# Input projection in three passes, the last of two k groups in one sum; modulation and gates ahead of it; weight offsets by kind

## The chip, the cores and the metric

The kernel runs on one core of a Trainium2 chip. The metric is the time that the device takes for one execution, in microseconds (us). Three runs of the kernel before took 1610.08, 1606.48 and 1610.29 us, a median of 1610.08. The engines are PE (TensorE, with PEld for its weight loads), DVE (VectorE), ACT (ScalarE), POOL (GpSimd) and SP (SyncE, which here only issues DMAs).

## The reference, cut to what matters

Two transformer blocks follow each other, for 256 tokens of width 2048, all in fp32. The change touches the first block only, apart from the place of weights in SBUF, which holds for all weights.

```
c_act = silu(c)
mod = c_act @ w_ada + b_ada                  # 2048 x 6144; c is one vector
shift, scale, gate = split(mod, 3)
h = rms(x) * (1 + scale) + shift             # 256 x 2048
proj = h @ w_in                              # 2048 x 8192
a_q, a_k, a_v, a_z, g_q, g_f, g_i, g_z = split(proj, 8)     # 1024 columns each
att = chunk_attention(a_q, a_k, a_v, bias) * silu(a_z)      # 8 heads, masked bias
hg  = hgrn2(g_q, g_f, g_i) * silu(g_z)                      # recurrence over tokens
x = x + gate * (concat(att, hg) @ w_out)
# second block: pool mixer, MLA, memory attention, w_o; then a gated FFN with 5632 columns
```

The sum over the 2048 rows of `w_in` is cut into four k groups of 512 rows. k group kg needs only the 512 columns kg of `h`, and so only these columns of `shift` and `scale`.

## The kernel before, in words

**Weights.** `load` (line 105) fetches a weight tile of 1 MB, 128 x 2048 fp32, into one of three buffers `wr`. `split_w` (line 112) cuts it, half a tile at a time, into a high part `wh` (ACT cast, line 120, three buffers) and a low part `wl` (DVE subtraction, line 121, two buffers). `tile_mm` (line 140) makes a job of each half tile: three matmuls for each product (line 165), high by high, high by low and low by high. There are three kinds. In T the weights are PE's stationary operand and 256 tokens move, in N the activations are stationary and 512 weight columns move, and in T2 (the FFN's gate and up weights and the like) the weights are stationary and 512 and 256 columns move. Two dummy tiles of 64 bytes, `pada` and `padb`, stand before and between `wh` and `wl` in SBUF; their addresses are the same for all three kinds.

**Order of the rest.** Everything that is not a weight job lies in two queues, `evq` and `bgq`, and is issued after each job until a budget of the phase is used up (`BUDGET`, line 34, `drain`); `AHEAD` says how many jobs are split ahead of the one whose matmuls are issued. So the program's order on each engine is set when it is built.

**Passes.** Twelve of the sixteen groups of `w_in` (512 columns each, `first_groups`, line 621) go through four passes, one for each k group: 48 tiles, 96 jobs. Each tile has PSUM banks of its own, and `part` (line 626) takes them to SBUF: for kg 0 an ACT copy (line 632), for kg 1 to 3 a DVE addition to what is there (line 634). `after` (line 811) runs behind each tile. It also advances the modulation of the next k group: two groups of 512 columns of `w_ada` (a scale and a shift, four 1 MB tiles each), `ada_steps` (line 402). Each tile has four chunks of 128 x 512 elements (`ada_tile`, line 368): "V" is one DVE operation, multiply and add (line 382), "P" is a product on ACT into `pts` (line 387) and an addition on POOL (line 388); the first chunk of a sum has no addition. `PAIR` = ("PPPP", "VVVV") gives the plan of the two groups. `ada_sum` (line 391) adds over partitions with small matmuls into a PSUM tile `ax`. At the end of a pass `make_h` (line 429) makes the next 512 columns of `h`, with their high and low parts.

**Gates.** The four groups 8 to 11 of `w_ada` (the block's `gate`) begin behind tile 10 of pass 3 (`GSTART`) with plans of three V and one P, the last all V. Their tiles are loaded with `load` into the weights' own `wr` buffers. They go on, a step per tile, through the stages gz (groups 14 and 15 of `w_in`), az (6 and 7) and out (`w_out`), where `need_y` (line 919) finishes them when needed.

**Beside it.** The recurrence of `hgrn2` (`level_inputs`, line 665, and on) begins once the four g_q and g_f groups are complete, in the fourth tile of pass 3; the attention heads (`chunk_heads`, line 640) once their groups are, from tile 8 on. A 128 x 128 mask `maskB` is added on POOL to each head's bias (line 646).

Of the kernel before, what the change touches and what calls it, by code (L numbers as in the profile page):

```python
# [28 lines left out]


# [28 lines left out]
def trunk_kernel(ctx, tc, a, out):  # L59
# [231 lines left out]
    maskB = sp_.tile([P, P], F32, tag="maskB", name="maskB")  # L291
    scanm = sp_.tile([P, T], F32, tag="scanm", name="scanm")
# [61 lines left out]
    n_ada = [0]  # L354

    def ada_buf(ng):
        if ng % 4 == 0 and ng < 8:
# [8 lines left out]
        return None
# [247 lines left out]
    def load_masks():  # L614
        for t, n in ((maskB, "maskB"), (scanm, "scanm")):
            SP.dma_start(t, a[n])
        hgf = slot("s7", [P, len(LEVELS), T])
        SP.dma_start(hgf, a["hgm"])
        later(1, lambda: V.tensor_copy(hgm, hgf))
# [188 lines left out]
    gates, xp = gate_steps(), []  # L808
    steps, hgt = [], []

    def after(kg, n, banks, ng, mode, dst, g, fin):
        for i, b in enumerate(banks):
            later(0.6, lambda i=i, b=b: part(kg, ng, mode, dst, g, b, i, fin), evq)
        if n == 0:
            steps.append(ada_steps((4 + kg + 1, kg + 1), PAIR) if kg < 3 else gates)
        if (n % 4 < EARLY and (kg < 3 or n >= GSTART)):
            next(steps[-1], None)
# [7 lines left out]
        if kg < 3 and n == 11:  # L825
            for _ in steps[-1]:
                pass
            make_h(kg + 1)
            if kg == 2:
                t = ytile("y0")  # L830
                hgt.extend((t[:, 0], t[:, 1]))
# [534 lines left out]
def _constants():  # L1366
# [11 lines left out]
    maskB = np.where(i[None, :] // 64 <= i[:, None] // 64, 0.0, NEG).astype(f)  # L1378
# [3 lines left out]
    for li, m in enumerate(LEVELS):  # L1382
# [7 lines left out]
        "maskC": maskC, "maskB": maskB, "scanm": scanm,  # L1390
# [60 lines left out]
```

## Time and profile before

| | |
|---|---|
| median of three runs | 1610.08 us (1606.48 to 1610.29) |
| profiled execution | 1608.93 us |
| its span | 1607.2 us |
| mean granted clock of PE | 0.991 |
| PE busy | 1549.3 us, 96% |
| DVE busy | 1157.4 us, 72% |
| ACT busy | 860.0 us, 54% |
| POOL busy | 366.9 us, 23% |
| DMA | 331.75 MB, mean 206 GB/s |

The span runs from the first to the last instruction of the profiled execution; 1.73 us of the execution's time lie outside it. By the first and last weight jobs of each part the stages are, in us from the start of the span: the memory's projection 10.2 to 88.2, pass 0 to 165.9, pass 1 to 235.5, pass 2 to 307.4, pass 3 to 394.0, gz to 472.0, az to 533.7, out to 638.6, then the second block, whose feed-forward runs from 882.7 to the end. A window by these bounds gives each engine's busy time in a stage. A busy PE is not PE at its peak, so its time is compared with what the number of jobs asks for.

### The profile page before, as it was taken

What the parts mean: (1) busy time and instruction counts of PE and PEld (TensorE: products, weight loads), DVE (VectorE), ACT (ScalarE), POOL (GpSimd) and SP (SyncE); (2) the same over time, 40 slices, a digit from 0 to 9 for tenths busy, and PEclk for the clock granted to TensorE, in tenths of its full rate; (3) what the DMA queues carried; (4) which work ended last, traced back from release to release, by engine and by line L of the source; (5) the groups of instructions that cost most, each with busy time, mean ns of one, the idle gap of its engine ahead of it and who ended that gap; (6) DMA issues with size and microseconds to landing.
All of it is one profiled execution on the core that took longest, in us unless ns stands there. A gap on an engine that the chain in (4) does not pass through costs nothing.

```text
span 1607.2 us, 24896 instructions
## 1 busy us (share of the span) xinstructions
PE 1549.3 (96%) x9754; PEld 1391.6 (87%) x9754; DVE 1157.4 (72%) x1610; ACT 860.0 (54%) x1254; POOL 366.9 (23%) x363
## 2 busy tenths in 40 slices
PE   5789999999899999999999999999999999999999
PEld 4677988878898999987999888888888888888887
DVE  7776999899997769567667766776676677545444
ACT  6366655564556745367645555555555555333332
POOL 3533435156653011512101211111111111000000
PEclk9899999999999999999999999999999999999999
DMA  9568878453655467443435555555555555556653
GB/s 386 211 245 300 339 286 318 180 183 132 229 191 213 175 243 264 158 163 136 153 132 184 184 188 202 187 194 200 186 200 192 190 204 183 203 190 208 206 189 131
DMA packets 50949, 331.75 MB, mean 206 GB/s; under 512 B 5648, under 2 KB 8080, under 8 KB 13456
## 3 DMA queue, kind: packets, MB, share of 16 engines
q1 hardware_dynamic: 50832, 330.17, 57.1%
q8 instruction: 76, 1.25, 0.3%
q14 instruction: 41, 0.34, 0.1%
HBM read 328.05 MB, written 2.10 MB: 205 GB/s over the span
## 4 chain that ended last, share of the span: by engine, by line
PE 83%; DVE 9%; POOL 2%; issue 2%; ACT 2%; DMA 1%; SPq 0%; DVEq 0%; ACTq 0%; POOLq 0%
PE mm L165 78%; DVE wl L121 4%; DVE acc L382 2%; POOL acc L388 1%; PE ax L724 1%; DMA wr<-in_w_mem_kv_dram 1%; PE ax L397 1%; ACT wh L120 1%; DMA wr<-in_w_ada_dram 1%; PE ax L253 1%; PE ax L522 1%; PE ax L223 0%; PE ax L514 0%; DVE s L314 0%; PE ax L650 0%
## 5 line engine op out<-in xcount | busy, mean ns | idle before, releaser
L121 DVE TENSOR_TENSOR wl<-wr,wh 128x1024 fp32r<-128x1024 f32 (+2 forms) x516 | 669.6, 1299 | 346.7 <-PE mm L165 308.9
L120 ACT CAST wh<-wr 128x1024 fp32r<-128x1024 f32 (+2 forms) x516 | 534.2, 1038 | 472.8 <-PE mm L165 392.2
L165 PE MATMUL mm<-h,wh 128*128 128x512 f32 (+1 forms) x2560 | 691.4, 343 | 0.4 <-ACT wh L120 0.4
L165 PE MATMUL mm<-h,wl 128*128 128x256 f32 x1984 | 553.5, 279 | 7.5 <-DVE wl L121 7.3
L165 PEld LDWEIGHTS mm<-h,wh 128*128 128x128 f32 x2560 | 444.1, 189 | 56.6 <-ACT wh L120 1.0
L165 PEld LDWEIGHTS mm<-h,wl 128*128 128x128 f32 x1984 | 374.2, 189 | 9.5 <-DVE wl L121 9.3
L165 PE MATMUL mm<-f,wh 128*128 128x512 f32 x704 | 239.4, 389 | 0.0
L165 PE MATMUL mm<-wh,h 128*128 128x512 f32 (+1 forms) x704 | 222.1, 391 | 0.0
L165 PE MATMUL mm<-f,wl 128*128 128x256 f32 x704 | 194.4, 276 | 0.0
L165 PE MATMUL mm<-y,wh 128*128 128x256 f32 x1024 | 185.3, 283 | 0.0
L165 PEld LDWEIGHTS mm<-y,wh 128*128 128x128 f32 x1024 | 156.6, 188 | 0.3 <-ACT wh L120 0.3
L165 PEld LDWEIGHTS mm<-wh,h 128*128 128x128 f32 x704 | 131.2, 188 | 29.1
L165 PEld LDWEIGHTS mm<-f,wh 128*128 128x128 f32 x704 | 132.1, 188 | 27.3
L165 PE MATMUL mm<-y,wl 128*128 128x256 f32 x512 | 143.9, 282 | 2.6 <-DVE wl L121 2.6
L165 PE MATMUL mm<-wl,h 128*128 128x512 f32 (+1 forms) x352 | 137.8, 392 | 3.4 <-DVE wl L121 3.4
L165 PEld LDWEIGHTS mm<-f,wl 128*128 128x128 f32 x704 | 132.2, 188 | 0.0
L1288 POOL TENSOR_TENSOR gp<-sg,R 128x256 f32<-128x256 f32 x44 | 35.9, 818 | 314.3 <-DVE sg L1287 314.3
L388 POOL TENSOR_TENSOR acc<-acc,pts 128x512 f32<-128x512 f32 x45 | 73.6, 1636 | 114.9 <-ACT pts L387 99.4
L165 PEld LDWEIGHTS mm<-y,wl 128*128 128x128 f32 x512 | 96.0, 188 | 3.4 <-DVE wl L121 3.4
L165 PEld LDWEIGHTS mm<-wl,h 128*128 128x128 f32 x352 | 66.3, 188 | 18.7 <-DVE wl L121 5.9
L165 PE MATMUL mm<-wh,s 128*128 128x512 f32 x128 | 45.4, 435 | 10.2 <-ACT wh L120 10.2
L634 DVE TENSOR_TENSOR s<-mm,s 128x512 f32<-128x512 f32 x72 | 49.0, 680 | 2.1 <-PE mm L165 1.8
(305 smaller groups left out, 1557.7 us busy)
## 6 DMA issues: line engine op xcount, KB each, us to landing
wr<-in_w_in_dram SPq DMA_DIRECT2D x76, 1024.0 KB, 4.9
wr<-in_w_gate_dram SPq DMA_DIRECT2D x44, 1024.0 KB, 4.7
wr<-in_w_up_dram SPq DMA_DIRECT2D x44, 1024.0 KB, 4.9
wr<-in_w_down_dram SPq DMA_DIRECT2D x40, 1024.0 KB, 4.9
y<-in_w_ada_dram SPq DMA_DIRECT2D x28, 1024.0 KB, 7.4
wr<-in_w_ada_dram SPq DMA_DIRECT2D x16, 1024.0 KB, 4.8
wr<-in_w_out_dram SPq DMA_DIRECT2D x16, 1024.0 KB, 4.7
wr<-in_w_o_dram SPq DMA_DIRECT2D x16, 1024.0 KB, 4.8
```

Of the source, the lines that this page charges most:

```text
L120: S.copy(hi, raw[:, k : k + n, :])
L121: V.tensor_tensor(lo, raw[:, k : k + n, :], hi.bitcast(F32), ALU.subtract)
L165: PE.matmul(d, l, r, start=st and i == 0, stop=sp and i == len(trip) - 1, skip_group_check=True)
L253: PE.transpose(ps[:, j * T + tb * P : j * T + tb * P + P], d[:, j, tb * P : tb * P + P], ident)
L382: V.scalar_tensor_tensor(accs[0], raw[:, k, :], cc, accs[0], ALU.mult, ALU.add)
L388: G.tensor_tensor(accs[1], accs[1], t, ALU.add)
L397: PE.matmul(ps[:, j * P : j * P + P], acc[:, j * P : j * P + P], ones, start=i == 0, stop=i == len(accs) - 1, skip_group_check=True)
L522: PE.matmul(po[:, :T], vblk(0), t[:, :T], start=True, stop=False, skip_group_check=True)
L634: V.tensor_tensor(d, b, d, ALU.add)
L724: PE.matmul(ps[:, j, b, :], k2[:, j, s], q2[:, j, s], start=True, stop=True)
L1288: G.tensor_tensor(gp[:, 2:], s, R3, ALU.mult)
```

## The change

The change has five parts.

1. *Three passes.* Passes kg 0 and kg 1 remain, 12 tiles each. Then tiles 0 to 2 run with kg 2, tiles 0 to 2 with kg 3, and each of tiles 3 to 11 with kg 2 and kg 3 one after the other. In these 24 tiles kg 2 and kg 3 add up in the same PSUM banks, and `part` takes only the whole sum: the 24 additions of kg 2 are gone. All 24 have the phase "pass3" with its budget of 2.0; pass 2 had 0.5 before.
2. *Modulation ahead.* `chain_steps` runs the modulations of k groups 1, 2 and 3 one after the other within the passes kg 0 and kg 1, two steps behind each fourth tile and one behind the others. Plans are PPPP and VVVV for the first, PPPP and VVPP for the second and third. `modulated` finishes what is left before a k group is first used.
3. *Gates ahead.* Behind the chain, one step per tile, with plan VVPP for all four and with two load buffers of their own in the tile `y1` (`gate_raw`) instead of `wr`. They must be complete before the first head is gated (`gate`, the new assertion), and the waits in `need_y` are gone.
4. *Masks.* The bias mask becomes an addition of a constant on a 64 x 64 corner; `scanm` is kept as bytes and cast beside `hgm`.
5. *Weight offsets by kind.* `wh` and `wl` are tiles of 1024 + 64 elements, and the weights begin at an offset set by `PLACE`. By the addresses that result, modulo 256 bytes and against the activations, before `wh` lies 64 bytes below and `wl` at 0 for all kinds; after, for N both lie at 0, for T both 64 bytes above, for T2 as before.

```diff
+PLACE = dict(N=dict(wh=0, wl=0), T=dict(wh=16, wl=16), T2=dict(wh=48, wl=0))
...
-GATES = ("VVVP", "VVVP", "VVVP", "VVVV")
-PAIR = ("PPPP", "VVVV")
-
-EARLY = 3
-GSTART = 10
+GATES = ("VVPP", "VVPP", "VVPP", "VVPP")
+PAIRS = (("PPPP", "VVVV"), ("PPPP", "VVPP"), ("PPPP", "VVPP"))
...
-        hi = wpool.tile([P, n, cw], F32R, tag="wh", name="wh", bufs=3)
...
-        lo = wpool.tile([P, n, cw], F32R, tag="wl", name="wl", bufs=2)
+        def place(tag, bufs):
+            o = PLACE[mode][tag]
+            t = wpool.tile([P, 1024 + 64], F32R, tag=tag, name=tag, bufs=bufs)
+            return t[:, o : o + n * cw].rearrange("p (k c) -> p k c", k=n)
+
+        hi, lo = place("wh", 3), place("wl", 2)
...
         raw = ada_buf(ng)
-        if raw is None:
-            raw = load(a["w_ada"][ng, kg], 4, 512)
-        else:
-            SP.dma_start(raw, a["w_ada"][ng, kg].rearrange("p (k c) -> p k c", k=4))
+        SP.dma_start(raw, a["w_ada"][ng, kg].rearrange("p (k c) -> p k c", k=4))
...
-                G.tensor_tensor(biases[h][:, P:T], biases[h][:, P:T], maskB, ALU.add)
+                G.tensor_scalar(biases[h][0:64, T - 64 : T], biases[h][0:64, T - 64 : T], NEG, None, ALU.add)
...
+    def chain_steps():
+
+        for kg in range(1, 4):
+            yield from ada_steps((4 + kg, kg), PAIRS[kg - 1])
+            make_h(kg)
+            done.add(f"m{kg}")
+            yield
+        t = ytile("y0")
+        hgt.extend((t[:, 0], t[:, 1]))
+        t = ytile("y1")
+        gate_raw.extend(t[:, i].rearrange("p (k a) t -> p k (a t)", k=4) for i in range(2))
+        done.add("chain")
...
     def after(kg, n, banks, ng, mode, dst, g, fin):
-        for i, b in enumerate(banks):
-            later(0.6, lambda i=i, b=b: part(kg, ng, mode, dst, g, b, i, fin), evq)
-        if n == 0:
-            steps.append(ada_steps((4 + kg + 1, kg + 1), PAIR) if kg < 3 else gates)
-        if (n % 4 < EARLY and (kg < 3 or n >= GSTART)):
-            next(steps[-1], None)
+        if kg != 2:
+            for i, b in enumerate(banks):
+                later(0.6, lambda i=i, b=b: part(kg, ng, mode, dst, g, b, i, fin), evq)
+        if "chain" in done:
+            next(gates, None)
+        else:
+            for _ in range(2 if n % 4 == 0 else 1):
+                next(chain, None)
...
-    for kg in range(4):
-        phase[0] = "pass3" if kg == 3 else "pass0"
-        for n, (ng, mode, dst, g, fin) in enumerate(first_groups):
-            banks = []
-            tile_mm(a["w_in"][ng, kg], 4 * kg, 4, 512, mode, banks, acth, True, True,
...
+    seq = [(n, kg) for kg in range(2) for n in range(12)]
+    seq += [(n, kg) for kg in (2, 3) for n in range(3)] + [(n, kg) for n in range(3, 12) for kg in (2, 3)]
+    open_banks, begun = {}, set()
+    for n, kg in seq:
+        phase[0] = "pass3" if kg >= 2 else "pass0"
+        ng, mode, dst, g, fin = first_groups[n]
+        banks = open_banks.setdefault((n, min(kg, 2)), [])
+        tile_mm(a["w_in"][ng, kg], 4 * kg, 4, 512, mode, banks, acth, kg < 3, kg != 2,
+                pre=(lambda kg=kg: modulated(kg)) if kg and kg not in begun else None,
...
     def need_y(kg):
         for j in range(4 * kg, 4 * kg + 4):
             ensure(f"y{j}")
-        if kg == 2 and not xp:
-            while "g9" not in done:
-                next(gates)
-                drain(0.1)
         if kg == 1 and not xp:
-            while "g10" not in done:
-                next(gates)
-                drain(0.1)
```

**Where instructions move.** First ACT in pass 0: `pts` are products of chunks (line 387 before, 380 after), CAST of `wh` is the weights' (line 120, now 119), COPY takes a tile's bank to `s` (line 632, now 625). Before:

```order
L387 ACTIVATE pts<-y_95,cact 128x512
L120 CAST wh<-wr 128x1024
L387 ACTIVATE pts<-y_95,cact 128x512
L632 COPY s_591<-mm 128x4x128
L120 CAST wh<-wr 128x1024
L632 COPY s_591<-mm 128x4x128
L120 CAST wh<-wr 128x1024
L387 ACTIVATE pts<-y_95,cact 128x512
L120 CAST wh<-wr 128x1024
L387 ACTIVATE pts<-y_95,cact 128x512 x3
```

After:

```order
L380 ACTIVATE pts<-y_94,cact 128x512 x4
L625 COPY s_588<-mm 128x4x128
L119 CAST wh<-wr 128x1024 x2
L625 COPY s_588<-mm 128x4x128
L380 ACTIVATE pts<-y_93,cact 128x512 x2
L380 ACTIVATE pts<-y_94,cact 128x512 x4
L119 CAST wh<-wr 128x1024 x2
L380 ACTIVATE pts<-y_93,cact 128x512 x2
L119 CAST wh<-wr 128x1024 x5
```

Single products and short runs stood between the casts; now runs of four and of six products of the two groups stand there with no cast between them.

Next POOL where the recurrence begins: R, `t_` and the 128 x 512 sums of `s_` are the recurrence's (lines 590 to 711 before, 583 to 704 after), and the additions of a buffer and `pts` are chunks (line 388, now 381). Before:

```order
L676 TENSOR_TENSOR R<-s_2858 128x2x64
L590 TENSOR_TENSOR s_593<-s_593,s_2857 128x512
L675 TENSOR_TENSOR R<-t_3000,s_2858 128x2x64
L692 TENSOR_TENSOR R<-s_2858 128x4x64
L590 TENSOR_TENSOR s_593<-s_593,s_2857 128x512 x3
L711 TENSOR_TENSOR y_2580<-s_592,R 128x2x128
L711 TENSOR_TENSOR y_2580<-s_592,R 128x4x64
```

After:

```order
L381 TENSOR_TENSOR y_2129<-y_2129,pts 128x512 x10
L583 TENSOR_TENSOR s_590<-s_590,s_2640 128x512 x2
L668 TENSOR_TENSOR R<-t_2878,s_2641 128x2x64
L669 TENSOR_TENSOR R<-s_2641 128x2x64
L685 TENSOR_TENSOR R<-s_2641 128x4x64
L381 TENSOR_TENSOR y_2129<-y_2129,pts 128x512 x2
L583 TENSOR_TENSOR s_590<-s_590,s_2640 128x512 x2
L381 TENSOR_TENSOR y_2129<-y_2129,pts 128x512 x2
L704 TENSOR_TENSOR y_2129<-s_589,R 128x2x128
```

Chunk additions of the gates now stand among the recurrence's first operations on POOL, where there were none.

Last SP, the DMA issues around the gates: `wr<-in_w_in_dram` is a tile of `w_in`, `in_w_ada_dram` one of the gates', `bias` the first heads' bias. Before:

```order
L645 DMA bias<-in_rel_dram 128x256 x2
L107 DMA wr<-in_w_in_dram 128x2048 x13
L107 DMA wr<-in_w_ada_dram 128x2048
L107 DMA wr<-in_w_in_dram 128x2048
L107 DMA wr<-in_w_ada_dram 128x2048
```

After:

```order
L107 DMA wr<-in_w_in_dram 128x2048 x4
L638 DMA bias<-in_rel_dram 128x256 x2
L107 DMA wr<-in_w_in_dram 128x2048
L367 DMA y_2130<-in_w_ada_dram 128x2048
L107 DMA wr<-in_w_in_dram 128x2048
```

The gates' tiles went into `wr`, in turn with the weights; now they go into a buffer of `y1` (here `y_2130`), the weights keep `wr` to themselves, and the first stands one weight tile behind the first `bias` instead of thirteen.

## Rows read from the trace of the kernel before

**Rows 1.** The page's first part: busy time, share, instructions
```profile
PE 1549.3 (96%) x9754; PEld 1391.6 (87%) x9754; DVE 1157.4 (72%) x1610; ACT 860.0 (54%) x1254; POOL 366.9 (23%) x363
```

**Rows 2.** Windows, passes 0 to 3, gz, az, out; us, engines, PEclk, DMA, GB/s
```profile
88.20:165.90 77.70, 72.55 (x409) 61.67 (x410) 56.90 (x63) 53.69 (x82) 27.84 (x20) 1.00 0.74 276
165.90:235.50 69.60, 69.60 (x402) 60.51 (x401) 65.22 (x74) 37.29 (x46) 25.99 (x16) 1.00 0.85 320
235.50:307.40 71.90, 70.14 (x401) 60.51 (x400) 63.38 (x77) 34.46 (x40) 26.21 (x17) 1.00 0.70 265
307.40:394.00 86.60, 82.37 (x506) 71.49 (x504) 82.20 (x125) 54.79 (x75) 41.51 (x42) 1.00 0.44 158
394.00:472.00 78.00, 71.46 (x571) 70.31 (x570) 74.71 (x108) 40.54 (x62) 47.83 (x46) 0.93 0.57 203
472.00:533.70 61.70, 58.56 (x487) 57.10 (x485) 48.56 (x88) 40.06 (x62) 19.63 (x17) 1.00 0.58 210
533.70:638.60 104.90, 103.04 (x848) 101.36 (x846) 82.82 (x138) 59.36 (x98) 13.36 (x15) 1.00 0.64 232
```

**Rows 3.** The same windows, instructions of tile ax alone; PE, PEld, DVE, ACT
```profile
235.50:307.40 71.90, 2.10 (x16) 2.09 (x16) 0.31 (x2) 0.00 (x0) 1.00 0.70 265
307.40:394.00 86.60, 15.32 (x120) 14.93 (x120) 9.13 (x15) 1.97 (x4) 1.00 0.44 158
394.00:472.00 78.00, 24.45 (x186) 22.63 (x185) 12.71 (x24) 3.25 (x6) 0.93 0.57 203
472.00:533.70 61.70, 14.59 (x102) 11.92 (x100) 5.11 (x12) 7.38 (x12) 1.00 0.58 210
533.70:638.60 104.90, 13.73 (x79) 11.34 (x76) 5.06 (x13) 5.90 (x14) 1.00 0.64 232
```

**Rows 4.** Pieces of the chain of waits: start us, us, what
```profile
356.33 1.78 PE ax L724 x16
...
418.55 2.83 PE mm L165 x24
```

**Rows 5.** Groups on DVE in pass 1: busy us, mean ns | idle before
```profile
L121 DVE TENSOR_TENSOR wl<-wr,wh 128x1024 fp32r<-128x1024 f32 x24 | 35.1, 1463 | 3.9 <-PE mm L165 1.6 <-issue 1.0 <-ACT wh L120 0.7
L634 DVE TENSOR_TENSOR s<-mm,s 128x512 f32<-128x512 f32 x22 | 15.0, 680 | 0.4 <-PE mm L165 0.4
L382 DVE SCALAR_TENSOR_TENSOR s<-y,cact,s 128x512 f32<-128x512 f32 x15 | 12.0, 802 | 0.1
```

**Rows 6.** The same view for POOL and for ACT
```profile
L388 POOL TENSOR_TENSOR acc<-acc,pts 128x512 f32<-128x512 f32 x16 | 26.1, 1634 | 41.9 <-ACT pts L387 41.1
...
L387 ACT ACTIVATE pts<-y,cact 128x512 f32<-128x512 f32 x15 | 10.4, 717 | 3.4 <-POOL acc L388 2.8 <-DMA y<-in_w_ada_dram 0.6
```

**Rows 7.** Timeline in pass 1: start us, us, engine line op [idle before]
```profile
186.50 1.22 DVE L121 TENSOR_TENSOR wl<-wr,wh 128x1024 fp32r<-128x1024 f32 x1
...
193.53 4.89 POOL L388 TENSOR_TENSOR acc<-acc,pts 128x512 f32<-128x512 f32 x3 [1.51 <-ACT pts L387]
...
197.17 2.33 DVE L121 TENSOR_TENSOR wl<-wr,wh 128x1024 fp32r<-128x1024 f32 x1 [0.67 <-ACT wh L120]
```

**Rows 8.** The chain of waits from gz to out, shares by line
```profile
by line: PE mm L165 50.8%; DVE acc L382 7.9%; DVE wl L121 6.9%; issue 4.1%; DMA wr<-in_w_ada_dram 3.9%; PE ax L724 2.7%; PE ax L397 2.7%; PE ax L650 2.2%; PE ax L253 2.0%; DVE y L725 1.6%; PE ax L522 1.5%; DVE h L314 1.3%; DVE x L908 1.1%; 
```

**Rows 9.** One line's instructions: ns min/median/max, first and last start
```profile
L388 POOL TENSOR_TENSOR acc<-acc,pts x45: 1276/1359/2212, 91.6 to 277.7; 128x512 f32<-128x512 f32 x45
```

**Rows 10.** Timeline of PE in pass 1, then in the feed-forward
```profile
210.26 0.63 PE L165 MATMUL mm<-wh,h 128*128 128x512 f32 x2
210.73 0.40 PE L165 MATMUL mm<-wl,h 128*128 128x512 f32 x1
...
1150.14 0.39 PE L165 MATMUL mm<-h,wh 128*128 128x512 f32 x1
1150.37 0.28 PE L165 MATMUL mm<-h,wl 128*128 128x256 f32 x1
1150.48 0.39 PE L165 MATMUL mm<-h,wh 128*128 128x512 f32 x1
```

More of the change, by code (lines that the diff above doesn't have):

```diff
@@ L290, in trunk_kernel @@
     sp_ = b1.enter_context(tc.tile_pool(name="s", bufs=1))
-    maskB = sp_.tile([P, P], F32, tag="maskB", name="maskB")
-    scanm = sp_.tile([P, T], F32, tag="scanm", name="scanm")
+    scanm = sp_.tile([P, T], U8, tag="scanm", name="scanm")
     hgm = sp_.tile([P, len(LEVELS), T], U8, tag="hgm", name="hgm")
@@ L614, in load_masks @@
     def load_masks():
[L615 to L619, printed above, removed]
+        n = len(LEVELS)
+        hgf = slot("s7", [P, n + 1, T])
+        SP.dma_start(hgf[:, 0:n, :], a["hgm"])
+        SP.dma_start(hgf[:, n, :], a["scanm"])
+        later(1, lambda: (V.tensor_copy(hgm, hgf[:, 0:n, :]), V.tensor_copy(scanm, hgf[:, n, :])))
     first_groups = [(10, "T", gk, 0, none), (11, "T", gk, 1, none), (8, "T", gq, 0, none),
@@ L795, in gate_acc2 @@
     def gate_acc2(ng):
-        if ng < 10:
-            return flat(hgt[0][:, 6:8, :])
-        return slot("s4", [P, 512]) if ng == 10 else tmp([P, 512], "acc2", 1)
+        return flat(hgt[0][:, 6:8, :])
     def gate_steps():
         for ng in range(8, 12):
-            while ng == 11 and not xp:
-                yield
             yield from ada_steps((ng,), (GATES[ng - 8],))
@@ L806, in gate_steps, with modulated @@
                 yield
-    gates, xp = gate_steps(), []
-    steps, hgt = [], []
-    def after(kg, n, banks, ng, mode, dst, g, fin):
-        for i, b in enumerate(banks):
-            later(0.6, lambda i=i, b=b: part(kg, ng, mode, dst, g, b, i, fin), evq)
-        if n == 0:
-            steps.append(ada_steps((4 + kg + 1, kg + 1), PAIR) if kg < 3 else gates)
-        if (n % 4 < EARLY and (kg < 3 or n >= GSTART)):
-            next(steps[-1], None)
+    def chain_steps():
[9 more added lines that the diff above has]
+        done.add("chain")
+    gates, chain, xp = gate_steps(), chain_steps(), []
+    hgt = []
+    def modulated(kg):
+        while f"m{kg}" not in done:
+            next(chain)
+        if kg == 3:
+            for _ in chain:
+                pass
+    def after(kg, n, banks, ng, mode, dst, g, fin):
+        if kg != 2:
[6 more added lines that the diff above has]
+                next(chain, None)
         if kg == 1 and n == 2:
@@ L824, in after @@
             when((f"aq{4 * i}", f"aq{4 * i + 2}", f"ak{4 * i}", f"ak{4 * i + 2}", f"in{4 + i}"), lambda: chunk_heads(i))
[L825 to L831, printed above, removed]
-    for kg in range(4):
-        phase[0] = "pass3" if kg == 3 else "pass0"
-        for n, (ng, mode, dst, g, fin) in enumerate(first_groups):
-            banks = []
-            tile_mm(a["w_in"][ng, kg], 4 * kg, 4, 512, mode, banks, acth, True, True,
-                    post=lambda kg=kg, n=n, banks=banks, ng=ng, mode=mode, dst=dst, g=g, fin=fin:
-                    after(kg, n, banks, ng, mode, dst, g, fin))
+    seq = [(n, kg) for kg in range(2) for n in range(12)]
[7 more added lines that the diff above has]
+                pre=(lambda kg=kg: modulated(kg)) if kg and kg not in begun else None,
+                post=lambda kg=kg, n=n, banks=banks, ng=ng, mode=mode, dst=dst, g=g, fin=fin:
+                after(kg, n, banks, ng, mode, dst, g, fin))
+        begun.add(kg)
     az, gz = [], []
@@ L1377, in _constants @@
     maskC[:, P:] = np.where(i[None, :] <= i[:, None], 0.0, NEG)
-    maskB = np.where(i[None, :] // 64 <= i[:, None] // 64, 0.0, NEG).astype(f)
     scanm = np.ascontiguousarray(np.broadcast_to((t % 64 != 0).astype(f), (P, T)))
@@ L1389, in _constants @@
         "ident": ident, "cs": np.ascontiguousarray(cs),
-        "maskC": maskC, "maskB": maskB, "scanm": scanm,
+        "maskC": maskC, "scanm": scanm,
         "hgm": hgm.reshape(P, len(LEVELS), T), "rcnt": np.ascontiguousarray(rcnt),
```

19 lines of the change are left out of this document (6 added, 13 removed).

## The prediction

> **What bounds the kernel now.** I read busy times first. PE is busy 96% of the span [rows 1], so nothing can be won but PE's own pace and its small gaps. Next the stretches by stage: passes 0 to 3 of the input projection, the two z stages (gz, az), and the first output projection (out) [rows 2]. From the first three DVE busy 57 to 65 of some 70 us is to be seen, in pass 3 and gz 82 of 87 and 75 of 78, in out 83 of 105. So the middle is where DVE is full. PE waits there less than the lengths suggest, because the stages also hold small matmuls of tile ax (turns, scores, recurrence): 2.1, 15.3, 24.5, 14.6 and 13.7 us from pass 2 to out [rows 3]. A job of 24 weight matmuls takes 2.83 us, and 16 ax matmuls 1.78 us, or 0.11 each [rows 4]. From pass 2 to out there are 24+24+16+16+32 = 112 jobs, 316 us. With 70 us of ax that is 386 of 403 us: 17 us of excess. The ax time itself holds waits and some half-speed clock (gz is granted 0.93 [rows 2]): by count, 503 ax records at 0.11 are 56 us, and the excess 31. So 17 to 31 us, say 26, is all that better scheduling can give back from pass 2 to out. Passes 0 and 1 have 24 jobs each, 68 us, against 77.7 and 69.6: pass 1 has nothing to give (PE busy for all of its 69.6 us [rows 2]) and much to lose.
>
> **Part A: three modulations within passes 0 and 1, two of them with six of eight chunks on ACT and POOL.** Before, each pass carried one modulation of 8 tiles, 16 chunks as ACT product and POOL add and 16 as one DVE operation. After, two passes carry three: 16+24+24 = 64 chunks by ACT and POOL, and 16+8+8 = 32 on DVE. Per pass that is 16 more ACT products, 14 more POOL adds (the first of a sum is no add) and no more DVE chunks. Prices from pass 1: product 0.717, add 1.634, wl (the low part of a weight half tile) 1.463, DVE chunk 0.802, PSUM add 0.680 [rows 5, 6]. POOL rises from 26 to 26 + 14 x 1.634 = 49 us per pass, ACT from 54 and 37 to 66 and 49. Neither exceeds 68 us. But DVE's wl takes 1.22 us when POOL is idle and 2.33 us while three POOL adds run [rows 7]. Pass 1 has 24 wl, 1.463 - 1.22 = 0.24 us each above the quiet price, for 16 adds. With 30 adds it will be 0.46, so 24 x 0.22 = 5 us more, as much for the chunks and the h splits together, and half a make_h (eight operations over half a chunk's columns, 0.4 each, 3.2 in all) 2 us. DVE comes to 65 + 5 + 4 + 2 = 76 us in pass 1 and 68 in pass 0. Pass 1 is 69.6 us and gets some 6.5 us longer. Pass 0 is hidden under its 77.7 us except where ACT stands: there products come in runs of four and six with no weight cast between (order in the part on the change), each product from the third on waits for a POOL add, and PE has two jobs, 5.6 us, in hand against 6 x 1.634 = 9.8 us; two or three such runs a pass cost about 2.5 us in pass 0, and in pass 1 fall in with DVE's excess. Part A: +9 us. Bounds: 0 if the buffered jobs cover it, +20 below. The 3.6 us of ax sums just move.
>
> The row shows that wl and POOL's adds delay each other. The Trainium skill, SBUF — State Buffer, section Who interferes with whom, says more: a VectorE operation with two SBUF inputs and a GpSimd operation that reads SBUF block each other for the whole instruction. The rows agree in kind: 2.33 against 1.22 us. What it would make of this is the first rival.
>
> **Part B: from pass 2 to out.** Groups of pass 2 are no longer added into SBUF: 24 additions of 0.68, 16.3 us of DVE. The modulation of pass 2 is gone (16 chunks, 12.8 us of DVE, and a make_h). The gates' 52 DVE chunks become 32, and all of them run in passes 2 and 3 instead of gz, az and out: 20 x 0.8 = 16 us less. DVE in sum is 45 to 50 us lighter of 352. None of this counts unless it stood on the path. The chain of waits from gz to out does show it there: DVE chunks of the gates 7.9% and the waits for w_ada tiles 3.9% of 245 us, 19 and 9.5 us [rows 8]. The latter come because the gates' tiles take the weights' own three buffers; after, they have two of their own, behind one weight load each, and in gz and az no w_ada is loaded at all. So up to 26 us can go. What is late next is the recurrence, DVE and POOL in turn, which now begins in the eighth of 24 tiles of passes 2 and 3 and is worked off there at budget 2.0. By the order all 28 of its predicated copies stand before gz's weights, where 8 did, and 18 of the gates' 28 POOL adds stand among its operations, where 9 did: 9 x 1.276 = 11.5 us more at least [rows 9] on an engine that is busy 42 of 87 in pass 3 and 48 of 78 in gz [rows 2], and the same DVE work in 24 jobs that took 36. I take half of the 26 us as kept: -12. Bounds: -26 and 0.
>
> **Part C: weight offsets by kind.** Only the matmuls' pace is at stake. By allocated addresses T2 (the feed-forward) keeps its distance of weights to activations modulo 256 bytes, so I hold it at its present price: a pair of 512 and 256 columns starts every 0.34 us, 0.443 ns a column, 113 ns for 256 and 227 for 512 [rows 10]. T runs 2.83 / 24 = 118 ns for 256 columns, N 0.47 / 2 = 235 for 512. T has 3264 matmuls (768 each in w_in, z, out and o, 192 in in2), N 1200 of full width. At T2's pace: 3264 x 5 + 1200 x 8 = 26 us less, the one end. At the other two N matmuls take 0.48, the next step that such a row can show, 0.24 each, +6. T2 itself has new addresses beyond 256 bytes; were it to fall to T's pace, 4% of 720 us, +28, which I keep for the range only. The nearest rows speak for little: before, N's wl stands at distance 0, which all of N gets, and is no faster than wh. I take a quarter of the gain, -6.
>
> Here the skill speaks against the edit: TensorE: Matmul & The Clock Gate, section What happens when you issue a matmul, has two independent read ports, so that loading the next weights takes nothing from the running matmul. By that no offset matters, and the sum would be 1606. The trace does not fit it well: 256 columns take 113 ns in T2 and 118 in T, at one granted clock of 1.00.
>
> **Other edits.** The mask for the bias becomes an addition on a 64 x 64 corner, eight of them, off the path; scanm as bytes adds a small cast beside the 1792-wide one in pass 1. Both hidden by POOL's idle time and PE's matmuls: 0, between -1 and +1.
>
> **Sum.** The profiled execution took 1608.93 us (span 1607.2). 1608.9 + 9 - 12 - 6 = 1599.9, so 1600. The median of the three runs is 1610.08, 0.1% above the profiled one, within the spread of what a measurement tells.
>
> **Rivals.**
> 1. *POOL and DVE exclude each other (slower).* Per pass 30 adds x 1.276, 24 wl x 1.22 and 16 chunks x 0.8 are 38 + 29 + 13 = 80 us, with the splits of h 85, on one shared path, where pass 1 with 16 adds needs 62 to 67 and has 69.6. From 18 adds a pass on it is the bound; there are 30. Then passes 0 and 1 take 85 to 88 us each with their start, +20, and B keeps only -4, because the gate adds meet the denser recurrence on the same path: 1608.9 + 20 - 4 - 6 = 1619. For it: wl at 2.33. Against it: pass 1 shows DVE and POOL busy for 65 and 26 us of 70 without PE ever waiting.
> 2. *The offsets do nothing.* 1608.9 + 9 - 12 + 0 to +6: 1606 to 1612. For it: N at distance 0.
> 3. *The offsets bring T and N to T2's pace.* 20 of the 26 us count, where PE sets the pace: 1608.9 + 9 - 12 - 20 = 1586.
> 4. *Passes 0 and 1 absorb the chain, and the DVE time that goes was all on the path.* 1608.9 + 0 - 24 - 6 = 1579. For it: POOL idle for 44 us of pass 1.
>
> **How the numbers follow.** About 0.3%, 5 us, is what a measurement here can tell from no change. Forecast 0.40 (1593 to 1606: 0.36 faster, 0.04 same); rival 1 0.17, slower; rival 2 0.16 (0.09 same, 0.07 slower); rival 3 0.14 and rival 4 0.10, faster; T2 harmed 0.03, slower. Faster 0.60, same 0.13, slower 0.27. The range goes from rival 4 to rival 1, 1578 to 1619; the likeliest case alone spans 1593 to 1606.
>
> **What would show it.** Right: pass 1 (96 jobs of passes taken as four blocks of 24) at about 76 us with wl near 1.7 us; pass 0 near 80; no wait for w_ada in the chain of gz and az; gz and az together below 125 us instead of 139.7, and passes 2 and 3 together, 158.5 us now, near 178, since they take in the recurrence's ax matmuls; T jobs below 2.83. Wrong: passes 0 and 1 unchanged or over 85 us; passes 2 and 3 together so long that gz's gain is given back; the feed-forward, 882.7 us to the end, other than 724 us; a job of T at 2.83 still.

## The result, and the profile after

The changed kernel takes 1655.31 us (median of four, 1653.11 to 1659.56) against 1610.18 before: the ratio is 1.0286, 95% interval 1.0266 to 1.0306. The forecast was 1600, range 1578 to 1619. The profiled execution took 1655.67 us, its span 1653.8, 46.6 more than before's.

By the first and last weight job of each part, as in the section on the profile before, in us (passes 2 and 3 together, since they are mixed now):

| part | before | after | difference | forecast |
|---|---|---|---|---|
| memory's projection | 78.0 | 75.8 | -2.2 | |
| pass 0 | 77.7 | 93.5 | +15.8 | 80 |
| pass 1 | 69.6 | 96.2 | +26.6 | 76 |
| passes 2 and 3 | 158.5 | 215.7 | +57.2 | 178 |
| gz, az | 139.8 | 106.9 | -32.9 | below 125 |
| out | 104.9 | 90.2 | -14.7 | |
| in2 to the end | 964.4 | 961.2 | -3.2 | |

The page's first part hardly differs from before's [rows 1]: DVE is even 14 us less busy than the 1157.4 there. Sums over the whole span don't show where the time went.

```profile
PE 1558.5 (94%) x9778; PEld 1397.7 (85%) x9778; DVE 1143.0 (69%) x1551; ACT 880.3 (53%) x1288; POOL 406.6 (25%) x396
```

The windows of the changed kernel: passes 0 and 1; passes 2 and 3 in four pieces of 12 jobs; then gz, az, out (columns as in [rows 2]).

```profile
86.10:179.50 93.40, 77.87 (x408) 65.01 (x408) 62.80 (x65) 60.35 (x94) 43.76 (x31) 0.93 0.66 253
179.50:275.70 96.20, 79.49 (x432) 67.69 (x433) 76.15 (x84) 50.50 (x67) 54.54 (x36) 0.93 0.71 277
275.70:312.60 36.90, 35.72 (x306) 35.29 (x305) 32.38 (x39) 24.72 (x31) 11.54 (x7) 1.00 0.89 338
312.60:363.00 50.40, 40.15 (x211) 33.98 (x210) 50.33 (x54) 34.02 (x46) 33.16 (x23) 0.93 0.65 237
363.00:432.20 69.20, 58.01 (x336) 49.60 (x335) 62.68 (x87) 31.87 (x52) 49.65 (x53) 0.98 0.45 162
432.20:491.30 59.10, 54.38 (x314) 46.45 (x314) 49.67 (x90) 29.73 (x46) 34.63 (x40) 0.98 0.30 107
491.30:553.10 61.80, 61.56 (x483) 59.11 (x482) 42.68 (x96) 38.97 (x77) 4.27 (x6) 0.99 0.51 184
553.10:598.30 45.20, 45.20 (x386) 45.20 (x385) 24.81 (x32) 24.59 (x31) 0.00 (x0) 1.00 0.53 187
598.30:688.50 90.20, 89.96 (x770) 89.76 (x770) 55.20 (x66) 44.51 (x55) 9.67 (x10) 1.00 0.55 196
```

In passes 0 and 1 PE is granted 0.93 instead of 1.00. In the second piece of passes 2 and 3 DVE is busy for 50.33 of 50.40 us. In az and out PE does weight jobs without a break, and DVE has some 40% of its time free.

The same groups as [rows 5, 6], now of pass 1 of the changed kernel:

```profile
L120 DVE TENSOR_TENSOR wl<-wr,wh 128x1024 fp32r<-128x1024 f32 x25 | 37.2, 1521 | 8.2 <-ACT wh L119 5.4 <-PE mm L164 2.8
L375 DVE SCALAR_TENSOR_TENSOR s<-y,cact,s 128x512 f32<-128x512 f32 x11 | 15.6, 1422 | 0.1
L627 DVE TENSOR_TENSOR s<-mm,s 128x512 f32<-128x512 f32 x23 | 15.5, 683 | 8.2 <-PE mm L164 8.2
...
L381 POOL TENSOR_TENSOR acc<-acc,pts 128x512 f32<-128x512 f32 x20 | 31.9, 1597 | 22.1 <-ACT pts L380 20.9
L381 POOL TENSOR_TENSOR s<-s,pts 128x512 f32<-128x512 f32 x11 | 19.5, 1770 | 7.4 <-ACT pts L380 7.0
```

There are 31 POOL additions instead of 16. A chunk on DVE takes 1.42 us instead of 0.80, wl 1.52 instead of 1.46, an addition on POOL 1.60 to 1.77. The addition from PSUM (L627) takes 0.683, where it took 0.680.

What PE waited for in passes 0 and 1 (us, times, longest), then ACT for POOL and DVE for ACT's casts:

```profile
PE mm L164 <- DVE wl L120: 15.9, 14, 2.9
PE ax L390 <- POOL acc L381: 12.6, 3, 5.4
PE ax L252 <- DVE memk L325: 2.4, 3, 0.9
PE mm L164 <- ACT wh L119: 1.3, 4, 0.5
...
ACT pts L380 <- POOL acc L381: 18.8, 21, 1.9
ACT pts L380 <- POOL s L381: 4.6, 4, 1.5
...
DVE wl L120 <- ACT wh L119: 22.0, 7, 5.5
```

PE's are 32 us; before, such waits came to 5.4 us in the two passes. The modulation's small sums (ax L390) stand in PE's order and wait for POOL's last addition. The chain of waits of pass 1 by line, after and then before:

```profile
by line: PE mm L164 40.9%; POOL acc L381 12.8%; POOL s L381 7.1%; issue 7.1%; DVE wl L120 6.7%; PE ax L390 6.6%; DMA y<-in_w_ada_dram 6.5%; DVE s L375 4.4%; DVE s L627 2.7%; ACT wh L119 2.2%; ACT pts L380 1.4%; DVE s L373 0.9%; ACT s L625 0
...
by line: PE mm L165 89.4%; DVE wl L121 4.7%; ACT h L437 2.5%; ACT wh L120 1.4%; PE ax L397 1.3%; DVE h L438 1.2%; DVE modT L399 0.1%; issue 0.1%; DVEq L121 0.1%
```

POOL's additions hold 20% of the chain, where none stood before.

Some five us of pass 1 in the timeline, and what they cost PE (start us, us, instruction, idle time before it):

```profile
233.54 7.56 POOL L381 TENSOR_TENSOR acc<-acc,pts 128x512 f32<-128x512 f32 x4 [1.04 <-ACT pts L380]
233.57 1.81 DVE L375 SCALAR_TENSOR_TENSOR s<-y,cact,s 128x512 f32<-128x512 f32 x1
...
235.31 1.28 DVE L627 TENSOR_TENSOR s<-mm,s 128x512 f32<-128x512 f32 x2
...
236.51 3.44 DVE L120 TENSOR_TENSOR wl<-wr,wh 128x1024 fp32r<-128x1024 f32 x2
...
237.77 0.50 PE L164 MATMUL mm<-wl,h 128*128 128x512 f32 x1 [2.85 <-DVE wl L120]
```

Four POOL additions, 1.27 us each when quickest, take 7.56 us. The DVE chunk that starts with the first takes 1.81, two wl take 3.44 together, and only the two additions from PSUM between them run at their usual 0.64. PE then waits 2.85 us for wl. A modulation's end, from the chain of waits:

```profile
249.66 1.63 POOL acc L381
...
251.35 1.27 POOL acc L381
...
252.67 1.53 PE ax L390 x8
...
254.31 1.24 DVE wl L120
...
255.59 6.51 PE mm L164 x18
```

POOL's last addition, the small sum, a wl, and then 18 weight matmuls in 6.51 us, 0.36 each, where N takes 0.23. PE had waited for 2.83 us before the small sum, and behind it runs a stretch at the lower of its two clock levels (the granted clock of these 6.5 us is 0.65 in the mean), so this wait cost more than its length.

### The profile page after: what moved, and what is told of

Same layout as the page of the kernel before. It is cut to its first block, busy times and chain, and to the rows that moved or that the text cites. A ratio compares the mean times of both kernels' runs of the same rounds, so it can differ in the third digit from the quotient of the medians.

```text
span 1653.8 us, 25005 instructions
## 1 busy us (share of the span) xinstructions
PE 1558.5 (94%) x9778; PEld 1397.7 (85%) x9778; DVE 1143.0 (69%) x1551; ACT 880.3 (53%) x1288; POOL 406.6 (25%) x396
## 4 chain that ended last, share of the span: by engine, by line
PE 81%; DVE 8%; POOL 4%; ACT 2%; issue 2%; DMA 1%; SPq 0%; DVEq 0%; ACTq 0%; POOLq 0%
PE mm L164 75%; DVE wl L120 3%; POOL acc L381 2%; PE ax L717 1%; ACT wh L119 1%; DVE acc L375 1%; PE ax L390 1%; DMA wr<-in_w_mem_kv_dram 1%; POOL s L381 1%; DMA y<-in_w_ada_dram 1%; PE ax L252 1%; PE ax L515 1%; PE ax L222 0%; ACT pts L380 0%; PE ax L643 0%
## 5 line engine op out<-in xcount | busy, mean ns | idle before, releaser
L164 PE MATMUL mm<-wh,h 128*128 128x512 f32 (+1 forms) x704 | 227.9, 396 | 0.4 <-ACT wh L119 0.3
L164 PE MATMUL mm<-y,wh 128*128 128x256 f32 x1024 | 180.7, 280 | 0.0
L381 POOL TENSOR_TENSOR acc<-acc,pts 128x512 f32<-128x512 f32 x45 | 68.1, 1513 | 68.6 <-ACT pts L380 66.1
L380 ACT ACTIVATE pts<-y,cact 128x512 f32<-128x512 f32 x92 | 63.8, 718 | 31.3 <-POOL acc L381 18.8
L381 POOL TENSOR_TENSOR y<-y,pts 128x512 f32<-128x512 f32 x28 | 45.8, 1635 | 40.1 <-ACT pts L380 25.8
```

Of the source, the lines that this page charges most:

```text
L164: PE.matmul(d, l, r, start=st and i == 0, stop=sp and i == len(trip) - 1, skip_group_check=True)
L380: S.mul(t, raw[:, k, :], cc)
L381: G.tensor_tensor(accs[1], accs[1], t, ALU.add)
```

## The experiments

Two theories of passes 0 and 1 were open: *order* (ACT stands in runs of products, the casts behind them) and *shared path* (POOL's additions and DVE's operations exclude each other). Of passes 2 and 3: the gates' chunks, or the denser recurrence by itself.

**1. The offsets alone, and all but the offsets.** The kernel before with `PLACE` and the smaller masks:

```diff
+PLACE = dict(N=dict(wh=0, wl=0), T=dict(wh=16, wl=16), T2=dict(wh=48, wl=0))
...
```

> The kernel before with the weight offsets by kind (and the smaller masks, without which the larger weight tiles do not fit), nothing else. The changed kernel's trace shows N matmuls of 512 columns starting every 228 ns instead of 234, and T matmuls of 256 columns partly every 113 instead of 118. If that is the offsets' doing: some 1200 N matmuls by 6 to 7 ns are 8 us, and between none and all of 3264 T matmuls by 4.5 ns are 0 to 15 us, so 1590 to 1602 us. If the new pace comes from something else in the changed kernel (longer gaps, other neighbours): 1610.

Measured: 1602.98 us, ratio 0.9957 (0.9942 to 0.9971). And the changed kernel without the offsets by kind:

```diff
-PLACE = dict(N=dict(wh=0, wl=0), T=dict(wh=16, wl=16), T2=dict(wh=48, wl=0))
+PLACE = dict(N=dict(wh=48, wl=0), T=dict(wh=48, wl=0), T2=dict(wh=48, wl=0))
```

> The changed kernel with the offset that T2 has for all three kinds, so that weights and activations stand to each other as before. If the offsets give the pace: N back to 234 ns, T to 118, and 8 to 15 us longer than the changed kernel, 1663 to 1670 us. If they do nothing: 1655.

Measured: 1662.97 us, 7.7 more than the changed kernel. So the offsets bring 6.6 us in the one kernel (with the smaller masks) and 7.7 in the other. By the starts of consecutive matmuls N takes 227 ns (median) with them and 235 without; of the 136 T jobs none runs at 113 ns a matmul without them, 77 with them in the kernel before, 61 in the changed one.

**2. One more job in hand.** In passes 0 and 1 two half tiles are split ahead:

```diff
-AHEAD = dict(mem=0, pass0=0, pass3=1, ...
+AHEAD = dict(mem=0, pass0=1, pass3=1, ...
```

> The changed kernel with one more half tile split ahead of the matmuls in passes 0 and 1 (AHEAD of that phase 1 instead of 0). Theory A, order: PE has only one job of 2.8 us in hand while ACT stands in a run of products, each waiting for a POOL addition, and the next weight casts are behind them in ACT's order. Then a second job in hand takes 20 to 30 us out of passes 0 and 1 (189.7 us): 1625 to 1635. Theory B, shared path: POOL and DVE slow each other so far that DVE and POOL are the bound: at most 5 us, 1650 to 1656. Theory C: PE stands in its own order before the small sums of the modulation, which wait for POOL's last addition (12.6 us in three waits): then no more than some 10 us go, about 1645.

Measured: 1653.77 us, passes 0 and 1 at 187.1 of 189.6. Pass 0 falls by 5.5 us, and pass 1 rises by 2.9. Order by itself is not it: the delay is not a hump that a job in hand would cover.

**3. Four buffers for products.** Two more, in the free half of the modulation's slot:

```diff
-                t = tmp([P, 512], "pts")
+                n_pts[0] += 1
+                t = more_pts[n_pts[0] % 4] if more_pts and n_pts[0] % 4 < 2 else tmp([P, 512], "pts")
...
```

> The changed kernel with four buffers for products in passes 0 and 1 instead of two, so that a run of four products does not stop ACT. Theory A (order): passes 0 and 1 fall by 15 to 30 us, the whole to 1625 to 1640. Theory B (shared path): POOL and DVE have the same work on it, at most 5 us go, 1650 to 1655.

Measured: 1649.35 us, passes 0 and 1 at 186.0. ACT's waits for POOL fall from 23.4 us to 2.6, and little comes of it; its waits for w_ada tiles rise from 4.6 to 12.0.

**4. POOL's additions as memsets.**

```diff
-                G.tensor_tensor(accs[1], accs[1], t, ALU.add)
+                if ng < 8 and phase[0] == "pass0":
+                    G.memset(t, 0.0)
+                    G.memset(t, 0.0)
+                    G.memset(accs[1][:, 0:192], 0.0)
+                else:
+                    G.tensor_tensor(accs[1], accs[1], t, ALU.add)
```

> The changed kernel, in passes 0 and 1 each POOL addition of a chunk replaced by three POOL memsets of about the same length in all (two of the product's buffer, one of 192 columns of the sum), so that the modulation's sums lack these chunks: work left out. ACT's products, their buffers and POOL's order stay, only the addition's two SBUF inputs go. Theory A, order (ACT's products wait for POOL, the casts stand behind them): passes 0 and 1 stay at 182 us or more of 189.6, the whole at 1648 or more. Theory B, shared path of POOL's additions and DVE's operations: wl falls from 1.47 us to about 1.22 and a DVE chunk from 1.2 to 0.75, passes 0 and 1 fall to 160 us or less, the whole to 1627 or less.

Measured: 1628.02 us, 27 less than the changed kernel, passes 0 and 1 at 160.6, both just above the bounds of the shared path and far below those of order. Passes 0 and 1 as windows, then DVE's groups in pass 1:

```profile
87.70:167.20 79.50, 73.44 (x411) 62.77 (x412) 49.44 (x66) 59.88 (x93) 39.98 (x97) 0.96 0.77 296
167.20:248.20 81.00, 73.73 (x433) 63.47 (x432) 60.39 (x84) 50.38 (x67) 39.20 (x88) 1.00 0.84 332
...
L120 DVE TENSOR_TENSOR wl<-wr,wh 128x1024 fp32r<-128x1024 f32 x25 | 29.7, 1220 | 8.3 <-ACT wh L119 5.2 <-issue 1.3 <-PE mm L164 1.2
L632 DVE TENSOR_TENSOR s<-mm,s 128x512 f32<-128x512 f32 x23 | 15.8, 688 | 15.0 <-PE mm L164 15.0
L375 DVE SCALAR_TENSOR_TENSOR s<-y,cact,s 128x512 f32<-128x512 f32 x11 | 8.2, 747 | 0.1
```

POOL is busy for 39 to 40 us a pass, in products' buffers as before, ACT has the same order, and yet wl takes 1.22 and a chunk 0.75 us. The length of POOL's work is not what hurts; that it reads SBUF beside DVE is. ACT's waits for POOL fall as well, from 23.4 to 6.7 us, but experiment 3 took nearly all of them away and won 3.6 us of the two passes. The addition from PSUM (L632) is as long as ever. This is what the Trainium skill, SBUF — State Buffer, section Who interferes with whom, states: a DVE instruction with two SBUF inputs and a GpSimd instruction that reads SBUF block each other, one with at most one SBUF input, outside the 2-port perf modes (as the addition from PSUM), or a GpSimd one that only writes does not. All three rows agree.

DVE's operations on one SBUF tensor and a column are not free of it. Here is `memk` in pass 0, of the changed kernel and then of experiment 5, where no chunk is added on POOL:

```profile
L325 DVE TENSOR_SCALAR memk<-memk,ssm 128x128 f32<-128x128 f32 x8 | 4.7, 664 | 1.2 <-POOL ssm L209 1.2
...
L325 DVE TENSOR_SCALAR memk<-memk,ssm 128x128 f32<-128x128 f32 x8 | 1.7, 278 | 1.5 <-POOL ssm L209 1.5
```

**5. All chunks on DVE.** Modulations and gates:

```diff
-GATES = ("VVPP", "VVPP", "VVPP", "VVPP")
-PAIRS = (("PPPP", "VVVV"), ("PPPP", "VVPP"), ("PPPP", "VVPP"))
+GATES = ("VVVV", "VVVV", "VVVV", "VVVV")
+PAIRS = (("VVVV", "VVVV"), ("VVVV", "VVVV"), ("VVVV", "VVVV"))
```

> The changed kernel with all chunks as one DVE operation, modulations and gates: no products on ACT, no additions on POOL. Passes 0 and 1: by theory A nothing holds the casts any more, DVE has 24 wl, 48 chunks, 8 or 16 splits of h, in pass 1 24 sums, 72 and 88 us at quiet prices: 155 to 165 us instead of 189.6; by theory B the same, since the additions of 1.27 us leave the path for DVE chunks of 0.75. So 1620 to 1632 if passes 2 and 3 stay. There theory B takes 28 times 1.27 - 0.75, 15 us, off as well, 1605 to 1617; if DVE by itself is the bound there, 28 chunks more on it cost 15 to 20 us, 1640 to 1650.

Measured: 1621.16 us, passes 0 and 1 at 162.7, passes 2 and 3 at 209.4. In passes 0 and 1 DVE alone does the 96 chunks 27 us faster than DVE, ACT and POOL did together. The gates' POOL additions are worth 6 us of passes 2 and 3, not the 15 of the one theory, nor a loss of 15 to 20.

**6. The gates as before.** From tile 10 of pass 3 on, in the old plan and through `wr`:

```diff
-            next(gates, None)
+            if kg == 3 and n >= GSTART:
+                next(gates, None)
...
```

> The changed kernel with the gates as before: from tile 10 of pass 3 on, three V and one P, loaded into the weights' own buffers. Theory A: the gates' chunks on DVE and POOL stand in the way of the recurrence, which now runs in the same 24 tiles; without them passes 2 and 3 fall from 215.7 to about 190 us, and gz to out rise from 197 to 225 to 235, since the gates stand there again: 1655 to 1667. Theory B: the recurrence is by itself too dense for these tiles, gates or not: passes 2 and 3 stay above 205, and the whole is at 1675 or more.

Measured: 1644.19 us, below what either theory had. Passes 2 and 3 fall to 182.0, by 33.7, and gz to out rise to 216.7, by 19.5. The four pieces of passes 2 and 3:

```profile
279.40:313.30 33.90, 33.90 (x289) 33.87 (x288) 21.92 (x29) 20.25 (x22) 1.23 (x1) 1.00 0.54 187
313.30:348.10 34.80, 33.68 (x194) 29.21 (x194) 29.65 (x40) 26.14 (x33) 15.00 (x10) 1.00 0.50 182
348.10:402.30 54.20, 51.58 (x304) 44.74 (x304) 47.41 (x73) 25.93 (x42) 35.54 (x44) 1.00 0.34 117
402.30:461.40 59.10, 53.31 (x311) 45.12 (x311) 52.78 (x90) 29.68 (x46) 34.88 (x40) 1.00 0.35 125
```

DVE is at 30 of 35 us in the second piece and 47 of 54 in the third, where the changed kernel has 50.33 of 50.40 and 62.68 of 69.20. So the gates went from places where DVE has room (in az and out 25 and 55 us of 45 and 90, with them gone) to a place where it has none.

**7. The kernel before with gates ahead.** From the first tile of pass 3 through buffers of their own, with the offsets:

```diff
-        if (n % 4 < EARLY and (kg < 3 or n >= GSTART)):
+        if n % 4 < EARLY or kg == 3:
...
+                t = ytile("y1")
+                gate_raw.extend(t[:, i].rearrange("p (k a) t -> p k (a t)", k=4) for i in range(2))
```

> The kernel before with the weight offsets (1603 us measured) and the gates, in their old plan of V and P, from the first tile of pass 3 on through two load buffers of their own, as in the changed kernel. If the waits for w_ada and the gates' chunks on the chain of gz to out (9.5 and 19 us) were the price of loading into wr and of their late place, and pass 3 has room for half of them: 1585 to 1597. If the gates cost as much in pass 3, beside the recurrence, as they give back later: 1600 to 1606. If they cost more there, as in the changed kernel (34 us against 20): 1610 to 1620.

Measured: 1618.22 us, 15 more than with the offsets alone. Counted to the end of pass 3's last weight matmul, passes 2 and 3 take 178.3 us instead of 154.9, and gz to out 238.1 instead of 246.6. The last six tiles of pass 3:

```profile
343.00:412.40 69.40, 55.09 (x277) 43.28 (x275) 67.44 (x99) 28.59 (x43) 39.49 (x40) 0.95 0.50 179
```

DVE is busy for 67.4 of 69.4 us. This holds without three passes and with the old plan of three V and one P: moved gates cost more than they give back in the old structure too.

**8. Both losses taken away.** The changed kernel with its modulations on DVE and the gates as before (the edits of 5, `PAIRS` only, and of 6):

> The changed kernel with all its modulations on DVE and the gates as before: the two edits that each took a part of the loss away. If they are independent: 1644.2 less 26.9 (passes 0 and 1 of the all-DVE run against the changed kernel's) is 1617, with passes 0 and 1 at 163 us, 2 and 3 at 182, gz to out at 217. If three modulations in two passes cost something beside POOL's additions, it is what stays: some 16 us above the 147 of passes 0 and 1 before. If the parts hang together (a later gate start meets a fuller DVE): 1625 or more.

Measured: 1620.82 us; passes 0 and 1 164.4, passes 2 and 3 181.8, gz to out 214.5. Within the spread of its runs (1616 to 1624) the parts are independent. What stays over the 147.3 of passes 0 and 1 before is 17 us. By experiment 5's trace DVE is busy for 147 of 163 us there, three modulations being 72 us of chunks; that this is the cause was not tested.

**9. T at other offsets.** In the kernel before with the offsets, for T alone:

```diff
-PLACE = dict(N=dict(wh=0, wl=0), T=dict(wh=16, wl=16), ...
+PLACE = dict(N=dict(wh=0, wl=0), T=dict(wh=32, wl=32), ...
```

> The kernel before with the weight offsets, those of T at 32 elements (128 bytes above the activations) instead of 16. With 16, 77 of 136 T jobs run at 113 ns a matmul and 59 at 118; with before's offsets none at 113. If any equal place of wh and wl gives that: about 1603. If 64 bytes were special: all 136 at 118, 8 us more than now in T, 1607 to 1610. If 128 bytes free all of them: 59 jobs of 24 by 4.5 ns, 6 us less, 1597.

Measured: 1607.60 us, none of 136 T jobs at 113 ns. The same with 0:

> As the run before, with T's offsets at 0, as N has them. Any equal place: 1603 and a like share of T jobs at 113 ns; 64 bytes special: 1607 to 1610, none at 113; 0 better: 1597.

Measured: 1609.10 us, none either. With 16 (64 bytes), then with 0, a run of T matmuls in pass 0 on PE's timeline:

```profile
100.74 0.39 PE L166 MATMUL mm<-h,wh 128*128 128x256 f32 x2
...
104.48 0.39 PE L166 MATMUL mm<-h,wh 128*128 128x256 f32 x2
```

```profile
100.72 0.40 PE L166 MATMUL mm<-h,wh 128*128 128x256 f32 x2
...
104.68 0.40 PE L166 MATMUL mm<-h,wh 128*128 128x256 f32 x2
```

Between the two rows shown lie 33 matmuls in either: 3.74 us with 64 bytes, 113 ns each, and 3.96 with 0, 120 each.

**10. Pass 0 of the kernel before without POOL.** With the offsets:

```diff
-            steps.append(ada_steps((4 + kg + 1, kg + 1), PAIR) if kg < 3 else gates)
+            steps.append(ada_steps((4 + kg + 1, kg + 1), PAIR if kg else ("VVVV", "VVVV")) if kg < 3 else gates)
```

> The kernel before with the weight offsets (1603.0 us measured), and in pass 0 alone all 32 chunks of the modulation on DVE. If POOL's additions and DVE share one path in pass 0 too (its chain of waits before holds 15.9% of POOL additions, wl takes 1.41 us there), 14 additions of 1.27 go from that path and 16 chunks of 0.75 come to it, and pass 0, 77.4 us, falls by 3 to 7: 1596 to 1600. If pass 0 is set by its start (norms of the memory's keys, first copies) or by DVE alone: no change, 1602 to 1605.

Measured: 1594.06 us, ratio 0.9899 (0.9881 to 0.9918): faster than both kernels, and the best here. Pass 0 with the offsets alone (window, DVE's wl, the chain of waits), then of this kernel:

```profile
88.00:165.40 77.40, 71.96 (x408) 62.22 (x409) 56.88 (x63) 53.28 (x82) 27.22 (x19) 0.98 0.74 277
...
L122 DVE TENSOR_TENSOR wl<-wr,wh 128x1024 fp32r<-128x1024 f32 x25 | 35.4, 1422 | 17.9 <-PE mm L166 8.3 <-ACT wh L121 5.8 <-issue 3.8
...
by line: PE mm L166 41.6%; DVE wl L122 14.2%; DMA y<-in_w_ada_dram 10.4%; POOL acc L388 9.0%; issue 6.5%; ACT wh L121 3.9%; DVE memk L327 3.7%; DVE s L382 3.2%; ACT pts L387 2.9%; DVE s L380 1.9%; DVE h L438 1.6%; DVE memv L338 1.0%; ACT h 
```

```profile
88.50:159.00 70.50, 69.21 (x409) 60.97 (x410) 59.11 (x79) 44.55 (x66) 5.48 (x5) 1.00 0.80 305
...
L122 DVE TENSOR_TENSOR wl<-wr,wh 128x1024 fp32r<-128x1024 f32 x25 | 30.5, 1222 | 8.5 <-PE mm L166 7.4 <-issue 1.0
...
by line: PE mm L166 92.3%; DVE wl L122 3.2%; PE ax L397 2.5%; DVE memk L327 1.7%; DVE memv L338 1.1%; issue 0.1%
```

Pass 0 falls from 77.4 to 70.5 us; the other 2 us of the gain of 8.9 were not looked into. With 16 chunks more on DVE, DVE is 2 us busier, since wl falls from 1.42 to 1.22 us, and the chain of waits is weight matmuls for 92% instead of 42%. The waits for w_ada tiles (10.4%) go too. The run takes products off ACT as well as additions off POOL, so it does not tell the two apart.

## Why the prediction was wrong

**Part A is the step that failed first**: +9 us, bounds 0 and +20, measured +42. The prediction saw the row that decides, wl at 2.33 us beside three POOL additions [rows 7], and made it a price on DVE's time alone, by extending pass 1's mean: 0.24 us per wl for 16 additions, 0.46 for 30, 4 us for the rest. It then let pass 1 grow by what DVE's sum grew, to 76 us, with ACT and POOL hidden beside it. That sum came out: DVE was busy for 76.15 us, and wl took 1.52 us, not even the 1.7 forecast. But the pass took 96.2 us, and DVE stood idle for 20 of them. What failed is the overlap. In the two passes DVE waited 22.0 us for ACT's casts, ACT 23.4 us for POOL's additions, and PE 32 us in all; on the shared path DVE's chunks went from 0.80 to 1.07 and 1.42 us, and POOL's additions took up to 2.2 us instead of 1.27. PE's clock adds to it: with two levels, the lower one half of the upper (1.2 and 2.4 GHz), a granted 0.93 of 93.5 and 96.2 us is an estimated 13 us at the lower one in each pass, where [rows 2] have 1.00. Experiment 4 shows 29 of the 42 us to go with the additions' reads of SBUF. The rest was not separated; one job in hand (2.5) and four buffers (3.6) take little off, and with all chunks on DVE 15 us stay.

**Rival 1 had the mechanism** and was given 0.17. Its sum on the shared path, 85 us a pass, is nearer to the 93.5 and 96.2 measured than the forecast's 80 and 76, and it had the point from which it decides (18 additions; there were 29 and 31). Its total, 1619, was still some 36 us short, since it gave passes 0 and 1 only 20 us more, and Part B a gain. Its argument against itself, that pass 1 showed no wait with DVE at 65 and POOL at 26 of 70 us [rows 2], was weak: 15 of DVE's 65 us are additions from PSUM, which don't use the path, so pass 1 just fitted in. Experiment 10 wins 7 us in pass 0, so the 77.7 us that [rows 2] has there for 68 us of jobs were not the cover that the prediction took them for: pass 0 hung on products and additions already.

**Part B**: -12 us, bounds -26 and 0, measured +9.7 (57.2 - 47.5). The gain came, and more than that: gz to out lost 47.5 us, of which 36 are recurrence matmuls that merely moved (ax is 53.7 us in passes 2 and 3, where it was 17.4 [rows 3]). This is the second step that failed, a term put at nothing: the prediction subtracted the gates' chunks from gz, az and out, and added nothing for them where they arrived, though [rows 2] gave DVE 82 of 87 us in pass 3, and though it named the recurrence, DVE and POOL in turn, as what is late next. Experiment 6 gives the two sides: 34 us lost, 19.5 gained; with the gates gone from there, passes 2 and 3 take 182 us, near the 178 forecast. The 24 additions that the common sum saves and the modulation that left pass 2 bring little together: with the gates as before, passes 2 to out take 398.7 us, and the kernel before with the offsets 401.5. Both of the prediction's signs of being wrong in these stages came: passes 0 and 1 over 85 us each, and gz's gain given back in passes 2 and 3.

**Part C** was -6 us, measured -6.6 in the one kernel and -7.7 in the other: right in size. T2's end of the bounds holds for N (227 ns) and for about half of T's jobs. That distance 0 was no faster in wl before was a poor witness; its neighbours wh stood 64 bytes off then, but that this is why was not tested. The Trainium skill, TensorE: Matmul & The Clock Gate, section Part 2: What happens when you issue a matmul, has two independent read ports; the prediction's own conclusion from it, that no offset matters, does not hold: T ran at 113 or 120 ns with nothing changed but 64 bytes of the weights' address. Other edits cost nothing that shows. T2 was not harmed: the feed-forward takes 714.9 us from its first job to its last in both.

So 1608.9 + 42 - 2 (memory's projection) + 10 - 3 (in2 to the end) = 1656, against 1655.67 of the profiled execution. The offsets' gain is within these parts, so the moves of work by themselves cost some 54 us.

## What to carry to other kernels

Before work goes to an engine that shares a path with another, add up what both do on it at quiet prices, and compare that with the stretch: here 62 to 67 us fitted into a pass of 69.6 without a wait, while 85 us against 68 us of jobs made passes of 93 and 96. Don't take a stage's length from its busiest engine's sum when the engines wait for each other in turn. Work that is moved off one stage's path has a price in the stage where it arrives; read that stage's busiest engine first, and charge the full time if it has no room. An operation's mean above its quiet time shows that a path is shared, not that it is full: wl took 1.41 us in pass 0 before and 1.42 after, and the pass grew by 16 us.

## What the runs showed of the hardware

- POOL additions with SBUF inputs and DVE operations with two SBUF inputs delay each other (four additions in 7.56 us instead of 5.08; chunk 1.42 us instead of 0.75), and DVE's `memk`, with one SBUF tensor, is delayed too (0.66 us instead of 0.28); DVE additions from PSUM (0.683 and 0.680) are free of it, and POOL memsets leave wl and chunks free (wl 1.22 us beside 39 us of them).
- The pace of matmuls depends on where the weights begin in SBUF. With the distances to the activations that the part on the change gives, T takes 117 to 121 ns for 256 columns at 0, 128 or mixed -64 and 0 bytes, and 113 or 118 at 64, one of the two for a whole job; N takes 235 ns for 512 columns at the mixed distances and 227 at 0. Only the weights were moved, so no run shows that the distance to the activations is what counts. In the changed kernel every change from 113 to 118 or back falls at an interruption of PE's run; az of the changed kernel, with no pause, stays at 118 throughout (45.2 us for 16 jobs, 2.83 each). Why a run falls into the one or the other was not settled.
- A stop of PE cost more than its length: behind a wait of 2.83 us and a small sum, 18 matmuls took 6.51 us instead of 4.1, at a granted clock of 0.65 in the mean.
